# The first input of a trunk kernel arrives in blocks among the first weights, and its norm is applied to products instead of to the input

## The chip, the cores and the metric

The kernel runs on one NeuronCore of a Trainium2 chip. The core has a matrix engine (TensorE, PE in the rows; PEld is its loading of stationary operands), a vector engine (VectorE, DVE), a scalar engine (ScalarE, ACT), GpSimd (POOL) and SyncE (SP), which here only issues DMAs. The metric is the device time of one execution, in microseconds (us); lower is better.

## The reference, cut to what matters

Two layers over 256 tokens of width 2048, all in fp32. Layer 0 mixes tokens by a gated DeltaNet, layer 1 by sparse attention, and each mixer is followed by a squared-ReLU MLP. The change touches the first lines of layer 0:

```python
u = x * rsqrt(mean(x * x, -1) + EPS) * norm_mix[0]
proj = u @ w_in                       # 2048 -> 12352
qkv, z, b, a = split(proj, ...)       # qkv: 16 + 16 + 32 heads of 128; z: 4096; b, a: 32 each
qkv = silu(causal_conv(qkv, conv_w))
beta = sigmoid(b)
g = -exp(a_log) * softplus(a + dt_bias)
o = chunk_gated_delta_rule(l2norm(q), l2norm(k), v, g, beta)
o = rms_norm(o, out_norm) * silu(z)
x = x + o @ w_out
```

The factor `rsqrt(mean(x * x) + EPS)` is one number per token, so it can be applied to the rows of `x`, or to the products `x @ w_in` of that token.

## The kernel before

Every fp32 matrix is cut into a high and a low part (`split`: ACT rounds to `xhi` or `whi`, DVE subtracts and leaves `xlo` or `wlo`), and each product is three matmuls, high by high, high by low and low by high (`mm3`).

**Weights.** `Stream` holds a list of items, one per 512 KB of weights in the order of use. SP's queue loads an item into one of four `raw` buffers; an item of a gate group is three DMAs (128, 128 and 256 columns). ACT and DVE split it into one of four pairs `whi` and `wlo`. `get` hands out an item and emits loads up to seven items ahead and splits up to three ahead.

**Where DMAs wait.** The build gives each DMA issued by SP or ACT one of eight semaphores in turn (DMAHW0 to DMAHW7 below), and a DMA that comes to a semaphore again waits until the DMA that had it before has landed.

**Start.** SP first loads `x` into `xin` (four DMAs of 128 x 1024), the identity `ident` and the small vectors, and then the first weights. ACT and DVE form the sums of squares, DVE the norm `rs`. `normalise` scales `xin` in place, 512 columns at a time. `first` is a generator: for each of 16 slices k of 128 columns, PE transposes both token blocks into an `aux` bank of PSUM (there are two, in turn), and ACT and DVE split the bank into `xhi` and `xlo`. It calls `normalise` for the next 512 columns on the way. Below, T*k* is the pair of transposes of slice k, A*k* the 12 matmuls of the first group on slice k (4 channel tiles x 3), and item *i* the i-th item of weights; items 0 to 7 are the first group's. `by_channel` with `ahead=3` puts T(k+3) ahead of Ak in PE's order.

**Groups.** 16 groups of two value heads follow. Each computes q, k and v by `by_channel` (8 items, 192 matmuls into two `acc` banks), copies them to `s` (ACT), computes its gate z by `by_token` (4 items, 96 matmuls), and adds the generator `delta` for the group to `Background`, which emits its steps among the next groups' matmuls, at times that a small model of the engines (`Pace`) decides at build time. In group 0, two items between q, k, v and z give the decay inputs (48 matmuls), and the generator `decays` turns them into `tokc`, for which PE transposes the tile `E`; `delta` of group 0 waits for it. There are four `acc` banks. The engines run what the build emitted, each in its own order.

Counted over the PE order, the first group's q, k and v are matmuls 1 to 192 into `acc`, the decay inputs 193 to 240, z of group 0 241 to 336, and group 1's q, k and v 337 to 528.

Of the kernel before, what the change touches and what calls it, by code (L numbers as in the profile page):

```python
# [127 lines left out]
class Stream:  # L128
# [11 lines left out]

    def get(self):
# [3 lines left out]
        while self.split < min(i + ahead + 1, len(self.items)) or self.loaded < min(i + self.loads + 1, len(self.items)):  # L145
            while self.loaded < min(self.split + self.loads - self.ahead, len(self.items)):
                (n, w), pieces, _ = self.items[self.loaded]
                raw = self.raw_pool.tile([P, 1024], F32, name="raw")
                view = raw[:, : n * w].rearrange("p (n w) -> p n w", n=n)
                for at, src in pieces:  # L150
                    self.sync.dma_start(out=at(view), in_=src)
                self.raw[self.loaded] = raw
                self.loaded += 1
# [20 lines left out]
def tile_hybrid_trunk(ctx: ExitStack, tc: tile.TileContext, a: dict, out: bass.AP):  # L174
# [219 lines left out]

    with tc.tile_pool(name="first", bufs=1) as fp:
        xin = fp.tile([P, 2, D], F32, name="xin")
        rows = fp.tile([P, P], F32, name="rows")
# [43 lines left out]

        normalise(0)

        def first():
# [612 lines left out]
```

## Time and profile before

| | |
|---|---|
| median of 3 runs | 2621.61 us (2621.15 to 2622.31) |
| the profiled execution's own time | 2621.18 us |
| its span in the profile | 2619.4 us |
| PE busy | 2583.4 us, 99% of the span |
| DVE busy | 1539.8 us, 59% |
| ACT busy | 1288.2 us, 49% |
| POOL busy | 332.9 us, 13% |

The own time is 1.8 us above the span. PE is busy nearly throughout, so what matters is when it starts, where it stands still, and what it executes.

### The profile page before, as it was taken

To read this page: it belongs to the slowest core of one execution; us is meant where nothing else is said; L and a number is where in the kernel's file an instruction comes from. 1 tells how busy PE (TensorE), PEld (TensorE's weight loads), DVE (VectorE), ACT (ScalarE), POOL (GpSimd) and SP (SyncE) were. 2 spreads that over 40 slices of the span, in tenths; PEclk is the share of its full clock that TensorE was granted. 3 is DMA by queue.
4 is the path that set the end of the run, shared out by engine and by line. 5 is a ranking of instruction groups with operands and counts; after the bars stand their busy time and mean duration, and the time that the engine had idled before them with its cause. 6 is when DMAs were issued, how large, how long until landed. Compare 5 with 4: busy or idle time off the path is not lost.

```text
span 2619.4 us, 52870 instructions
## 1 busy us (share of the span) xinstructions
PE 2583.4 (99%) x21795; PEld 2356.7 (90%) x21795; DVE 1539.8 (59%) x2308; ACT 1288.2 (49%) x1992; POOL 332.9 (13%) x674
## 2 busy tenths in 40 slices
PE   7999999999999999999999999999999999999997
PEld 7999999999987899988899988898899988999886
DVE  5777677676764555554455545576555544555544
ACT  5555555555554444443344444566544433444443
POOL 0344434343441000000000000000000000000000
PEclk9999999999999999999999999999999999999999
DMA  6655455555544566666656666644566666666664
GB/s 191 187 142 146 132 150 143 154 142 142 148 165 154 183 184 195 194 199 193 194 177 188 195 192 187 185 129 147 176 192 193 194 193 193 191 187 186 193 193 137
DMA packets 325394, 455.95 MB, mean 174 GB/s; under 512 B 18280, under 2 KB 159840, under 8 KB 324768
## 3 DMA queue, kind: packets, MB, share of 16 engines
q1 hardware_dynamic: 321888, 443.85, 56.8%
q10 hardware_dynamic: 2928, 7.37, 0.8%
q8 instruction: 171, 2.80, 0.4%
q0 software_dynamic: 336, 1.34, 0.1%
q14 instruction: 71, 0.58, 0.1%
HBM read 450.37 MB, written 2.13 MB: 173 GB/s over the span
## 4 chain that ended last, share of the span: by engine, by line
PE 66%; DVE 1%; ACT 0%; issue 0%; ACTq 0%; DVEq 0%
PE acc L78 64%; PE aux L78 1%; PE pk L78 1%; DVE wlo L78 0%; DVE p L78 0%; DVE score L78 0%; ACT whi L78 0%; ACT h L78 0%; ACT acc L78 0%; DVE m L78 0%; DVE nm L78 0%; DVE h L78 0%; ACT p L78 0%; DVE rs_t L78 0%; DVE rs_u L78 0%
## 5 line engine op out<-in xcount | busy, mean ns | idle before, releaser
L78 DVE TENSOR_TENSOR wlo<-raw,whi 128x1024 fp32r<-128x1024 f32 x838 | 1024.4, 1229 | 870.6 <-ACT whi L78 862.7
L78 ACT CAST whi<-raw 128x1024 fp32r<-128x1024 f32 x838 | 873.9, 1049 | 844.1 <-PE acc L78 813.6
L78 PE MATMUL acc<-whi,h 128*128 128x512 f32 x2816 | 887.6, 392 | 2.1 <-ACT acc L78 2.1
L78 PE MATMUL acc<-xhi,whi 128*128 128x256 f32 x3088 | 876.1, 284 | 0.3 <-ACT whi L78 0.3
L78 PE MATMUL acc<-xhi,wlo 128*128 128x256 f32 x3088 | 860.7, 279 | 0.5 <-DVE wlo L78 0.5
L78 PE MATMUL acc<-xlo,whi 128*128 128x256 f32 x3088 | 861.1, 279 | 0.0
L78 PEld LDWEIGHTS acc<-whi,h 128*128 128x128 f32 x2816 | 528.8, 188 | 111.8 <-ACT acc L78 2.9
L78 PEld LDWEIGHTS acc<-xhi,wlo 128*128 128x128 f32 x3088 | 585.2, 190 | 0.8 <-DVE wlo L78 0.8
L78 PEld LDWEIGHTS acc<-xhi,whi 128*128 128x128 f32 x3088 | 581.3, 188 | 4.6 <-ACT whi L78 0.7
L78 PEld LDWEIGHTS acc<-xlo,whi 128*128 128x128 f32 x3088 | 582.2, 189 | 0.2
L78 PE MATMUL acc<-wlo,h 128*128 128x512 f32 x1408 | 548.3, 389 | 0.0
L78 PEld LDWEIGHTS acc<-wlo,h 128*128 128x128 f32 x1408 | 264.6, 188 | 52.7
L78 PE MATMUL acc<-whi,xhi 128*128 128x256 f32 (+2 forms) x576 | 173.7, 302 | 0.0
L78 PE MATMUL acc<-whi,xlo 128*128 128x256 f32 (+2 forms) x576 | 166.5, 289 | 0.0
L78 PE MATMUL acc<-wlo,xhi 128*128 128x256 f32 (+2 forms) x576 | 166.2, 289 | 0.0
L78 POOL DMA_DIRECT2D gain<-in_norm_final x1 | 0.6, 639 | 979.1 <-ACT p L78 979.1
L78 POOL TENSOR_SCALAR E<-R,tokc 128x128 f32<-128x128 f32 x96 | 88.1, 931 | 249.0 <-DMA R<-gl_dram 226.8
L78 DVE SCALAR_TENSOR_TENSOR y<-s,cw,y 128x255 f32<-128x255 f32 (+2 forms) x192 | 93.5, 488 | 41.4 <-ACT y L78 36.8
L78 PEld LDWEIGHTS acc<-whi,xhi 128*128 128x128 f32 x576 | 108.0, 187 | 3.6
L78 PEld LDWEIGHTS acc<-wlo,xhi 128*128 128x128 f32 x576 | 108.3, 188 | 1.3
L78 PEld LDWEIGHTS acc<-whi,xlo 128*128 128x128 f32 x576 | 108.1, 188 | 1.2
L78 POOL TENSOR_TENSOR h<-h,gain 128x512 f32<-128x512 f32 x8 | 10.1, 1284 | 776.9 <-ACT acc L78 776.9
(245 smaller groups left out, 1944.3 us busy)
## 6 DMA issues: line engine op xcount, KB each, us to landing
raw<-in_mlp_w_up SPq DMA_DIRECT2D x256, 512.0 KB, 4.4
raw<-in_mlp_w_down SPq DMA_DIRECT2D x256, 512.0 KB, 4.3
raw<-in_dn_w_in SPq DMA_DIRECT2D x66, 512.0 KB, 4.2
raw<-in_dn_w_in SPq DMA_DIRECT2D x256, 128.0 KB, 2.8
raw<-in_dn_w_in SPq DMA_DIRECT2D x128, 256.0 KB, 3.2
raw<-in_dn_w_out SPq DMA_DIRECT2D x64, 512.0 KB, 3.8
raw<-in_dsa_w_out SPq DMA_DIRECT2D x32, 512.0 KB, 4.1
raw<-in_dsa_w_uq SPq DMA_DIRECT2D x16, 512.0 KB, 3.7
```

Source lines behind the costliest of these rows:

```text
L78: r = f(*args, **kwargs)
```

## The change

`x` stays as it is. It is loaded as four blocks of 512 columns for all 256 tokens, each as one more DMA ahead of the weights of items 0, 1, 3 and 5. `ident` and the first 16 vector rows go to ACT's queue, the other seven vector loads come after item 3 on SP's. `first` transposes raw slices as soon as their block has been issued, and forms the norm afterwards: four `squares` steps, the sum, `rsqrt`, a diagonal `dg`, and a matmul of `ones` with `dg` that lays the norm along the columns of `rs_row`. `s` is then a product with `rs_row` (DVE, from PSUM) instead of a copy (ACT), in all 16 groups; z takes half the norm as the scale of its tanh; one more POOL product per group puts the norm into `f`; `decays` gets two more products. Group 0's decay and z matmuls now come before `bg.drain()`. Two runs of matmuls of `ones` with itself (12 and 8, `warm_up`) whose results are not used are added to PE.

```diff
+    def fetch(self):
+        while self.loaded < min(self.split + self.loads - self.ahead, len(self.items)):
+            (n, w), pieces, _ = self.items[self.loaded]
+            raw = self.raw_pool.tile([P, 1024], F32, name="raw")
+            view = raw[:, : n * w].rearrange("p (n w) -> p n w", n=n)
+            for at, src in pieces:
+                self.sync.dma_start(out=at(view), in_=src)
+            self.raw[self.loaded] = raw
+            self.loaded += 1
+
...
-            ws.add((2, 512), [
+            blocks = [slice(c * 512, c * 512 + 512) for c in range(4) if g == 0 and k // 2 == max(0, 2 * c - 1)]
+            ws.add((2, 512), [((lambda v, c=c: xin[:, :, c]), x_rows[:, :, c]) for c in blocks] + [
...
-        quarters = [(tb, slice(c * 1024, c * 1024 + 1024)) for c in range(2) for tb in range(2)]
-        for tb, s in quarters:
-            sync.dma_start(out=xin[:, tb, s], in_=a["x"][0, tb * P:tb * P + P, s])
-        sync.dma_start(out=ident, in_=a["consts"][:, 0:P])
-        dve.memset(rows, 0.0)
+        def warm_up(n):
+            warm = aux()
+            for _ in range(n):
+                pe.matmul(warm[:, 0:P], lhsT=ones, rhs=ones, start=True, stop=True)
+
+        warm_up(12)
+        act.dma_start(out=rows[0], in_=a["norm_mix"][0].rearrange("(n p) -> n p", p=P))
+        act.dma_start(out=ident, in_=a["consts"][:, 0:P])
+        pool.dma_start(out=cwr, in_=a["dn_conv_w"][0].rearrange("t (c p) -> (t c) p", p=P).rearrange("(n q) p -> q n p", q=P))
+        pool.dma_start(out=upper, in_=a["consts"][:, P:2 * P])
+        pool.dma_start(out=fine, in_=a["consts"][:, 2 * P:].rearrange("p (n c) -> p n c", c=B))
+
...
+        sq8 = small_tile(8, "sq8")
+        ws.fetch()
...
-            sync.dma_start(out=rows[at:at + n, :], in_=src.rearrange("(n p) -> n p", p=P))
+            if at:
+                sync.dma_start(out=rows[1][at - 16:at - 16 + n, :], in_=src.rearrange("(n p) -> n p", p=P))
...
-        sq4 = small_tile(4, "sq4")
-        for n, (tb, s) in enumerate(quarters):
-            junk = fp.tile([P, 1024], F32, name="junk", bufs=2)
-            if n % 2 == 0:
-                act.activation(junk, xin[:, tb, s], AF.Square, accum_out=sq4[:, n:n + 1])
-            else:
-                dve.scalar_tensor_tensor(junk, xin[:, tb, s], 1.0, xin[:, tb, s], op0=OP.mult, op1=OP.mult, accum_out=sq4[:, n:n + 1])
-        rs = small_tile(2, "rs")
-        sq = small_tile(2, "sq")
-        dve.tensor_tensor(sq, sq4[:, 0:2], sq4[:, 2:4], op=OP.add)
-        dve.tensor_scalar(sq, sq, 1.0 / D, EPS, op0=OP.mult, op1=OP.add)
-        rsqrt(rs, sq, 2)
-        tp = aux()
-        pe.transpose(tp[:, 0:P], rows, ident)
-        act.copy(vecs, tp[:, 0:72])
-
...
+        def vectors(i, s):
+            tp = aux()
+            n = s.stop - s.start
+            pe.transpose(tp[:, 0:n], rows[i], ident[0:n, 0:n])
+            act.copy(vecs[:, s], tp[:, 0:n])
+
+        vectors(0, slice(0, 16))
+
+        def squares(c):
             s = slice(c * 512, c * 512 + 512)
-            act.activation(xin[:, 0, s], xin[:, 0, s], AF.Copy, scale=rs[:, 0:1])
-            dve.tensor_scalar(xin[:, 1, s], xin[:, 1, s], rs[:, 1:2], None, op0=OP.mult)
-
-        normalise(0)
+            junk = fp.tile([P, 2, 512], F32, name="junk", bufs=2)
+            act.activation(junk[:, 0], xin[:, 0, s], AF.Square, accum_out=sq8[:, c:c + 1])
+            dve.scalar_tensor_tensor(junk[:, 1], xin[:, 1, s], 1.0, xin[:, 1, s], op0=OP.mult, op1=OP.mult,
+                                     accum_out=sq8[:, 4 + c:5 + c])
...
             for k in range(KD):
+                while ws.loaded <= max(0, k // 4 * 2 - 1):
+                    yield
...
                 ready.add(("x0", k))
-                if k % 4 == 1 and k < 12:
-                    normalise(k // 4 + 1)
-                yield
+                yield
+            for c in range(4):
+                squares(c)
+                yield
+            sq = small_tile(2, "sq")
+            dve.tensor_reduce(sq, sq8.rearrange("p (b c) -> p b c", b=2), axis=AX.X, op=OP.add)
+            dve.tensor_scalar(sq, sq, 1.0 / D, EPS, op0=OP.mult, op1=OP.add)
+            rsqrt(rs0, sq, 2)
+            dg = fp.tile([P, 2, P], F32, name="dg")
+            for tb in range(2):
+                dve.tensor_scalar(dg[:, tb], ident, rs0[:, tb:tb + 1], None, op0=OP.mult)
+            yield
+            t = aux()
+            pe.matmul(t[:, :T], lhsT=ones, rhs=dg.rearrange("p b c -> p (b c)"), start=True, stop=True)
+            act.copy(rs_row, t[:, :T])
+            yield
...
+            vectors(1, slice(16, 72))
...
         bg.step()
+        warm_up(8)
         first_banks = by_channel(8, x_part, "x0", ahead=3)
+        first_ba = by_channel(2, x_part, "x0", n_ct=1)[0]
+        first_zo = by_token(4, x_part, "x0", n_cols=256)
         bg.drain()
...
+        dve.tensor_scalar(rs_half, rs0, 0.5, None, op0=OP.mult)
...
-            act.activation(ba[64:96], ps[64:96, :T], AF.Tanh, scale=0.5)
+            dve.tensor_tensor(ba[64:96], ps[64:96, :T], rs_row[64:96], op=OP.mult)
+            act.activation(ba[64:96], ba[64:96], AF.Tanh, scale=0.5)
...
-            dve.tensor_scalar(xa, ps[q, :T], par[q, 1:2], None, op0=OP.add)
+            dve.tensor_tensor(xa, ps[q, :T], rs_row[q], op=OP.mult)
+            dve.tensor_scalar(xa, xa, par[q, 1:2], None, op0=OP.add)
...
             pool.tensor_tensor(pair(f), pair(f), rep(sc), op=OP.mult)
+            pool.tensor_tensor(pair(f), pair(f), rep(rs0), op=OP.mult)
...
-                act.copy(s[:, 2 * c:2 * c + 2].rearrange("p n t -> p (n t)"), banks[c])
+                dve.tensor_tensor(s[:, 2 * c:2 * c + 2], banks[c].rearrange("p (n t) -> p n t", n=2),
+                                  rs_row.unsqueeze(1).to_broadcast([P, 2, T]), op=OP.mult)
             if g == 0:
-                bg.add(decays(by_channel(2, x_part, "x0", n_ct=1)[0]))
-            zo = by_token(4, x_part, "x0", n_cols=256)
...
-                act.activation(zg[:, b], zo[b], AF.Tanh, scale=0.5)
+                act.activation(zg[:, b], zo[b], AF.Tanh, scale=rs_half[:, b:b + 1])
```

On SP's queue, ahead of the first weights before the change, and between item 3 (`raw_141`) and item 5 (`raw_189`) after it. Before:

```order
L411 DMA rows_98<-in_norm_mlp 16x128 [waits DMAHW0_49]
L411 DMA rows_98<-in_dsa_q_norm 4x128 [waits DMAHW1_49]
L411 DMA rows_98<-in_dsa_kv_norm 2x128 [waits DMAHW2_49]
L411 DMA rows_98<-in_dsa_kidx_norm 1x128 [waits DMAHW3_49]
L411 DMA rows_98<-in_dn_out_norm 1x128 [waits DMAHW4_49]
L151 DMA raw_162<-in_dn_w_in 128x2x128 [waits DMAHW5_49]
L151 DMA raw_162<-in_dn_w_in 128x2x128 [waits DMAHW6_49]
L151 DMA raw_162<-in_dn_w_in 128x2x256 [waits DMAHW7_49]
```

After:

```order
L147 DMA raw_141<-in_dn_w_in 128x2x256 [waits DMAHW0_49]
L436 DMA rows56_106<-in_norm_mlp 16x128 [waits DMAHW1_49]
L436 DMA rows56_106<-in_norm_mix 16x128 [waits DMAHW2_49]
L436 DMA rows56_106<-in_norm_mlp 16x128 [waits DMAHW3_49]
L436 DMA rows56_106<-in_dsa_q_norm 4x128 [waits DMAHW4_49]
L436 DMA rows56_106<-in_dsa_kv_norm 2x128 [waits DMAHW5_49]
L436 DMA rows56_106<-in_dsa_kidx_norm 1x128 [waits DMAHW6_49]
L436 DMA rows56_106<-in_dn_out_norm 1x128 [waits DMAHW7_49]
L147 DMA raw_181<-in_dn_w_in 128x2x128 [waits DMAHW0_49,DVE_49]
L147 DMA raw_181<-in_dn_w_in 128x2x128 [waits DMAHW1_49]
L147 DMA raw_181<-in_dn_w_in 128x2x256 [waits DMAHW2_49]
L147 DMA xin_104<-in_x 128x2x512 [waits DMAHW3_49]
```

Before, all of `x` and the small vectors stood ahead of the first weights. Now the small vectors stand behind item 3, and the first load of item 4 (`raw_181`) waits for the semaphore of item 3's last load.

On DVE's queue, the two weight splits of items 4 and 5 and what stands behind them, before and after. Before (`raw_182` and `raw_190` are items 4 and 5; `aux_297` and `aux_314` hold T7 and T8):

```order
L78 TENSOR_TENSOR wlo_286<-raw_182,whi_285 128x1024 [waits DMAHW2_49,DMAHW3_49,DMAHW1_49,Activation_49]
L78 TENSOR_TENSOR wlo_292<-raw_190,whi_291 128x1024 [waits DMAHW5_49,DMAHW4_49,DMAHW6_49,PE_49,Activation_49]
L78 SCALAR_TENSOR_TENSOR xlo_93<-aux_297,vecs_85,xhi_92 128x256 [waits Activation_49]
L78 SCALAR_TENSOR_TENSOR xlo_93<-aux_314,vecs_85,xhi_92 128x256 [waits Activation_49]
L78 TENSOR_TENSOR wlo_332<-raw_237,whi_331 128x1024 [waits DMAHW1_49,DMAHW0_49,DMAHW7_49,PE_49,Activation_49]
L78 SCALAR_TENSOR_TENSOR xlo_93<-aux_337,vecs_85,xhi_92 128x256 [waits Activation_49]
```

After (`raw_181` and `raw_189` are items 4 and 5; `aux_295` and `aux_312` hold T7 and T8):

```order
L78 TENSOR_TENSOR wlo_284<-raw_181,whi_283 128x1024 [waits DMAHW1_49,DMAHW2_49,DMAHW0_49,Activation_49]
L78 TENSOR_TENSOR wlo_290<-raw_189,whi_289 128x1024 [waits DMAHW5_49,DMAHW4_49,DMAHW6_49,PE_49,Activation_49]
L78 SCALAR_TENSOR_TENSOR xlo_93<-aux_295,vecs_85,xhi_92 128x256 [waits Activation_49]
L78 SCALAR_TENSOR_TENSOR xlo_93<-aux_312,vecs_85,xhi_92 128x256 [waits Activation_49]
L78 TENSOR_TENSOR wlo_330<-raw_237,whi_329 128x1024 [waits DMAHW1_49,DMAHW0_49,DMAHW7_49,PE_49,Activation_49]
```

The order of splits is the same in both: item 5's split stands ahead of slice 7's. Only the in-place scaling (`xin`) is gone. T9 uses the `aux` bank that T7 had, and so waits for slice 7's split.

On DVE's queue at the end of group 0 after the change (`raw_565` is item 16; `acc_175` and `acc_176` are the two banks of the first group; before, ACT copied them as soon as the 192 matmuls were done):

```order
L78 TENSOR_TENSOR wlo_614<-raw_453,whi_613 128x1024 [waits DMAHW2_49,PE_49,Activation_49]
L78 TENSOR_TENSOR wlo_646<-raw_491,whi_645 128x1024 [waits DMAHW4_49,DMAHW5_49,DMAHW3_49,Activation_49]
L78 TENSOR_TENSOR wlo_688<-raw_527,whi_687 128x1024 [waits DMAHW6_49,DMAHW0_49,DMAHW7_49,PE_49,Activation_49]
L78 TENSOR_TENSOR wlo_720<-raw_565,whi_719 128x1024 [waits DMAHW2_49,DMAHW3_49,DMAHW1_49,Activation_49]
L78 TENSOR_SCALAR rs_half_99<-rs0_98 128x2
L78 TENSOR_TENSOR s_757<-acc_175,rs_row_100 128x512
L78 TENSOR_TENSOR s_757<-acc_176,rs_row_100 128x512
L78 SCALAR_TENSOR_TENSOR zg_760<-zg_760,acc_612 128x256 [waits Activation_49] x2
```

The products that free the two banks now stand behind item 16's split, and group 1's first matmuls take these two banks. On PE, the transposes of `E` stand behind `acc` matmul 444 before (inside group 1's q, k and v) and behind 576 after (inside its z); the matmul with `dg` stands behind 276, and the transposes of `cwr` and of the other vectors behind 288 (`cwr`: 168 before). The first products of `delta` for groups 0 to 4 stand 144, 132, 108, 72 and 42 `acc` matmuls later than before; from group 5 on they stand where they stood.

## Rows read from the trace of the kernel before

**Rows 1.** PE's waits over the whole span: total us, times, longest.
```profile
PE aux L78 <- DVE rs_t L78: 13.0, 1, 13.0
...
PE aux L78 <- DVE E L78: 1.5, 1, 1.5
```

**Rows 2.** Timeline of the start: start us, length us, engine, what, idle before and releaser.
```profile
0.73 1.81 SPq L401 DMA_DIRECT2D xin<-in_x  x4
...
5.34 0.31 SPq L411 DMA_DIRECT2D rows<-in_norm_mlp  x1
5.34 1.06 ACT L78 ACTIVATE junk<-xin 128x1024 f32<-128x1024 f32 x1 [3.33 <-DMA xin<-in_x]
...
10.79 0.22 SPq L411 DMA_DIRECT2D rows<-in_dsa_kidx_norm  x1
...
11.36 45.74 SPq L151 DMA_DIRECT2D raw<-in_dn_w_in  x42
...
20.04 0.58 PE L78 MATMUL acc<-xhi,wlo 128*128 128x256 f32 x1 [0.47 <-DVE wlo L78]
```

**Rows 3.** Windows of the start: last column GB/s moved, before it DMA share.
```profile
0.00:5.00 5.00, 0.00 (x0) 0.00 (x0) 0.31 (x2) 1.28 (x1) 3.23 (x9) 1.00 0.54 160
...
15.00:20.00 5.00, 3.03 (x10) 1.83 (x10) 2.78 (x6) 4.16 (x8) 0.00 (x0) 1.00 0.97 275
...
5.00:9.00 4.00, 0.00 (x0) 0.00 (x0) 1.23 (x2) 1.15 (x2) 0.00 (x0) 1.00 1.01 371
...
12.30:15.00 2.70, 0.44 (x1) 0.18 (x1) 2.25 (x14) 0.43 (x2) 0.00 (x0) 1.00 0.88 229
...
17.00:20.00 3.00, 1.91 (x6) 1.11 (x6) 2.36 (x5) 3.00 (x6) 0.00 (x0) 1.00 1.08 325
```

**Rows 4.** Timeline of PE: neighbours at 25 us, and fp32 products at 243 us.
```profile
24.69 0.41 PE L78 MATMUL acc<-xhi,whi 128*128 128x256 f32 x1
...
24.90 0.36 PE L78 MATMUL acc<-xlo,whi 128*128 128x256 f32 x1
...
25.69 0.28 PE L78 MATMUL acc<-xhi,wlo 128*128 128x256 f32 x1
...
243.80 0.71 PE L78 MATMUL aux<-r,Tt 128*128 128x128 f32 x4
...
244.27 0.36 PE L78 MATMUL acc<-xhi,whi 128*128 128x256 f32 x1
```

**Rows 5.** Timeline of PE: T8 and T9, and `acc` matmuls 192 and 193.
```profile
30.11 0.38 PE L78 MATMUL aux<-wide,xin 128*128 128x128 f32 x2
...
31.74 0.38 PE L78 MATMUL aux<-wide,xin 128*128 128x128 f32 x2
...
47.52 0.28 PE L78 MATMUL acc<-xhi,wlo 128*128 128x256 f32 x1
47.63 0.28 PE L78 MATMUL acc<-xhi,whi 128*128 128x256 f32 x1
```

**Rows 6.** Timeline of PE: `acc` matmul 444, and the transposes of `E`.
```profile
76.73 0.28 PE L78 MATMUL acc<-xhi,wlo 128*128 128x256 f32 x1
78.53 0.44 PE L78 MATMUL aux<-wide,E 128*128 128x128 f32 x2 [1.52 <-DVE E L78]
```

**Rows 7.** Groups by form up to 700 us (`h<-acc`: 700 to 1640): busy us, mean ns of one, idle before and releasers.
```profile
L78 DVE TENSOR_TENSOR wlo<-raw,whi 128x1024 fp32r<-128x1024 f32 x186 | 229.4, 1238 | 112.7 <-ACT whi L78 106.0 <-DMA raw<-in_dn_w_in 5.1 <-DMA R<-gl_dram 0.9
...
L78 DVE SCALAR_TENSOR_TENSOR xlo<-aux,vecs,xhi 128x256 fp32r<-128x256 f32 x16 | 7.2, 479 | 3.4 <-ACT xhi L78 3.4
...
L78 ACT CAST whi<-raw 128x1024 fp32r<-128x1024 f32 x186 | 193.2, 1047 | 62.9 <-PE acc L78 50.8 <-DVE E L78 4.8 <-ACT y L78 4.0
...
L78 DVE TENSOR_TENSOR h<-acc,h 128x512 f32<-128x512 f32 x8 | 5.0, 682 | 0.0
...
L78 POOL TENSOR_TENSOR f<-f,sc 128x4 f32<-128x4 f32 x12 | 2.4, 201 | 0.9
```

**Rows 8.** One window of the groups: busy us of PE, PEld, DVE, ACT, POOL.
```profile
310.00:410.00 100.00, 100.00 (x1371) 94.14 (x1365) 68.55 (x155) 57.37 (x122) 42.59 (x93) 1.00 0.52 144
```

More of the change, by code (lines that the diff above doesn't have):

```diff
@@ L145, in get @@
         while self.split < min(i + ahead + 1, len(self.items)) or self.loaded < min(i + self.loads + 1, len(self.items)):
[L146 to L153, printed above, removed]
+            self.fetch()
             if self.split >= min(i + ahead + 1, len(self.items)):
@@ L213, in tile_hybrid_trunk @@
     QO, KO, VO, ZO, BO = 0, 2048, 4096, 8192, 12288
+    x_rows = a["x"][0].rearrange("(b p) d -> p b d", p=P)
     for g in range(DN_G):
         for k in range(0, KD, 2):
-            ws.add((2, 512), [
+            blocks = [slice(c * 512, c * 512 + 512) for c in range(4) if g == 0 and k // 2 == max(0, 2 * c - 1)]
+            ws.add((2, 512), [((lambda v, c=c: xin[:, :, c]), x_rows[:, :, c]) for c in blocks] + [
                 (lambda v: v[:, :, 0:128], w_in[:, k:k + 2, KO + g * 128:KO + g * 128 + 128]),
@@ L392, in two_chunks, with vec @@
         return [by_token(2, h_part(tiles), key, outs=o, k0=nk - 4) for o in outs]
+    carry = ExitStack()
+    carried = carry.enter_context(tc.tile_pool(name="carried", bufs=1))
+    tokc = carried.tile([P, 2, P], F32, name="tokc")
+    rs0 = carried.tile([P, 2], F32, name="rs0")
+    rs_half = carried.tile([P, 2], F32, name="rs_half")
+    rs_row = carried.tile([P, T], F32, name="rs_row")
     with tc.tile_pool(name="first", bufs=1) as fp:
         xin = fp.tile([P, 2, D], F32, name="xin")
-        rows = fp.tile([P, P], F32, name="rows")
+        rows = [fp.tile([n, P], F32, name=f"rows{n}") for n in (16, 56)]
         cwr = fp.tile([P, 2, P], F32, name="cwr")
-        quarters = [(tb, slice(c * 1024, c * 1024 + 1024)) for c in range(2) for tb in range(2)]
-        for tb, s in quarters:
-            sync.dma_start(out=xin[:, tb, s], in_=a["x"][0, tb * P:tb * P + P, s])
-        sync.dma_start(out=ident, in_=a["consts"][:, 0:P])
-        dve.memset(rows, 0.0)
+        def warm_up(n):
[8 more added lines that the diff above has]
+        pool.dma_start(out=fine, in_=a["consts"][:, 2 * P:].rearrange("p (n c) -> p n c", c=B))
+        def vec(name, i=0):
+            return vecs[:, VEC[name] + i:VEC[name] + i + 1]
+        sq8 = small_tile(8, "sq8")
+        ws.fetch()
         at = 0
@@ L410, in tile_hybrid_trunk @@
             n = src.shape[0] // P
-            sync.dma_start(out=rows[at:at + n, :], in_=src.rearrange("(n p) -> n p", p=P))
+            if at:
+                sync.dma_start(out=rows[1][at - 16:at - 16 + n, :], in_=src.rearrange("(n p) -> n p", p=P))
             VEC[name] = at
             at += n
-        pool.dma_start(out=cwr, in_=a["dn_conv_w"][0].rearrange("t (c p) -> (t c) p", p=P).rearrange("(n q) p -> q n p", q=P))
-        pool.dma_start(out=upper, in_=a["consts"][:, P:2 * P])
-        pool.dma_start(out=fine, in_=a["consts"][:, 2 * P:].rearrange("p (n c) -> p n c", c=B))
@@ L418, in vec @@
-        def vec(name, i=0):
-            return vecs[:, VEC[name] + i:VEC[name] + i + 1]
-        sq4 = small_tile(4, "sq4")
-        for n, (tb, s) in enumerate(quarters):
-            junk = fp.tile([P, 1024], F32, name="junk", bufs=2)
-            if n % 2 == 0:
-                act.activation(junk, xin[:, tb, s], AF.Square, accum_out=sq4[:, n:n + 1])
-            else:
-                dve.scalar_tensor_tensor(junk, xin[:, tb, s], 1.0, xin[:, tb, s], op0=OP.mult, op1=OP.mult, accum_out=sq4[:, n:n + 1])
@@ L428, in tile_hybrid_trunk @@
-        rs = small_tile(2, "rs")
-        sq = small_tile(2, "sq")
-        dve.tensor_tensor(sq, sq4[:, 0:2], sq4[:, 2:4], op=OP.add)
-        dve.tensor_scalar(sq, sq, 1.0 / D, EPS, op0=OP.mult, op1=OP.add)
-        rsqrt(rs, sq, 2)
-        tp = aux()
-        pe.transpose(tp[:, 0:P], rows, ident)
-        act.copy(vecs, tp[:, 0:72])
-        def normalise(c):
+        def vectors(i, s):
[3 more added lines that the diff above has]
+            act.copy(vecs[:, s], tp[:, 0:n])
@@ L461, in tile_hybrid_trunk @@
         bg.step()
+        warm_up(8)
         first_banks = by_channel(8, x_part, "x0", ahead=3)
+        first_ba = by_channel(2, x_part, "x0", n_ct=1)[0]
+        first_zo = by_token(4, x_part, "x0", n_cols=256)
         bg.drain()
-    tokc = const.tile([P, 2, P], F32, name="tokc")
     GLM, BETA, GL = 32, 64, 96
@@ L719, in tile_hybrid_trunk @@
             for c in range(2):
-                act.copy(s[:, 2 * c:2 * c + 2].rearrange("p n t -> p (n t)"), banks[c])
+                dve.tensor_tensor(s[:, 2 * c:2 * c + 2], banks[c].rearrange("p (n t) -> p n t", n=2),
+                                  rs_row.unsqueeze(1).to_broadcast([P, 2, T]), op=OP.mult)
             if g == 0:
-                bg.add(decays(by_channel(2, x_part, "x0", n_ct=1)[0]))
-            zo = by_token(4, x_part, "x0", n_cols=256)
+                bg.add(decays(first_ba))
+            zo = by_token(4, x_part, "x0", n_cols=256) if g else first_zo
             if g > 2:
@@ L738, in tile_hybrid_trunk @@
     spare[:] = [None, "pk0", None, "pk1"]
+    carry.close()
     res = ctx.enter_context(tc.tile_pool(name="res", bufs=1, reuse_waits="tile"))
```

## The prediction

> **What bounds the kernel now.** I read the waits of PE first. PE is busy for 99% of the span, as the table has it; 13.0 us of waiting lie ahead of its first instruction, and 1.5 us at the tile `E`, in group 1 [rows 1]. In the groups PE is busy for 100 of 100 us while DVE has 31 us to spare [rows 8]. So this change can gain what PE loses at the start, and it loses wherever it stops PE anew.
>
> The timeline of the start shows why PE is late. SP loads `x` from 0.73 us on, then the small vectors, and issues the first weights only at 11.36 us [rows 2]. The eight semaphores do that: SP's next vector load is issued at 5.34 us, in the moment in which ACT's wait for the first piece of `x` ends, so a DMA that takes a semaphore over waits for the landing of the one before. PE's stream without gaps begins at 20.04 us [rows 2], and it begins at half rate: neighbours start 0.21 us apart up to 24.90 us, against 0.11 us later [rows 4, 5]. These are the 1.2 and the 2.4 GHz level; the column of the granted clock says 1.00 throughout [rows 3] and doesn't show it. T9 then starts at 31.74 us, and the first matmul behind group 0's q, k and v at 47.63 us [rows 5].
>
> **Where T9 goes.** I place the new start by T9, because what follows it is known: from T9 to 47.63 us are 15.89 us without a wait [rows 5]. In that stretch stands the pair of `cwr`, which moves away. From 47.63 to 76.73 us PE starts 251 matmuls, 0.116 us each [rows 5, 6]; a slice takes 31.74 - 30.11 = 1.63 us, so a pair of transposes costs 1.63 - 12 x 0.116 = 0.24 us. Without it, T9 to the end of q, k, v is 15.65 us.
>
> T9 waits for the split of slice 7, which stands on DVE behind the split of item 5, so it waits for item 5 to land. How late is that?
>
> Bytes: a block of `x` and an item are 524 KB each; `cwr`, `upper`, `fine`, `ident` and 16 vector rows are 370 KB by their shapes. Up to 5 us the queues moved 160 GB/s, that is 800 KB; later 371 GB/s (`x` in long rows) and 325 GB/s (weights in short rows, queue full) [rows 3]. Blocks now have rows of 2 KB, between the two kinds; I take 325.
>
> - Item 3's last load comes after 3 blocks and 4 items: 3670 + 370 - 800 = 3240 KB, 10.0 us at 325 GB/s, so at 15.0 us. The same count for the fourth piece of `x` before gives 9.5 us (800 KB, then 371 GB/s); it landed at 10.79 us, when SP's waiting load went out [rows 2]. Last pieces trail by up to 1.3 us; I take 0.7, hence 15.7 us.
> - Only then does SP issue item 4, since seven small loads hold the other semaphores. The queue is empty, and it starts as it did before at 11.36 us: nothing for a while, then 229 GB/s from 12.3 to 15.0 us, 620 KB in 3.6 us [rows 2, 3]. Items 4, 5 and the last block are 1570 KB: 620 by 19.3 us, 950 more at 325 GB/s, so item 5 lands at 22.2 us.
> - Behind it: its cast 1.05, its subtraction 1.24, slice 7's `xlo` 0.48 us [rows 7], and some 0.2 us of hand-offs, my estimate. T9 at 25.2 us.
>
> PE is there earlier. T4 waits in the same way for item 1 (2 blocks, 2 items: 1670 KB after 5 us, 10.1 us, with the trailing about 10.6) and starts some 3.0 us later, at 13.6; five slices on, PE is ready for T9 at 13.6 + 5 x 1.63 = 21.8 us and waits 3.4 us. What the first `warm_up` costs lies ahead of that. An fp32 product of 128 columns costs 0.235 us at the fast level (two in 0.47 us, four records) [rows 4], about 0.43 at the slow one: 12 of them run from about 1 to 6.2 us, 0.9 us past the landing of block 0 (as the first piece before, 5.3 us). The 8 others cost 1.9 to 3.5 us. At worst A0 ends at 14.5 us instead of before 13.6; the wait at T9 swallows it. Without that wait it would cost the 0.9 us. So the warm-ups are worth their faster clock only up to T9.
>
> Then q, k, v end at 25.2 + 15.65 = 40.85 us, **6.8 us earlier** than 47.63. The bounds: at 371 GB/s T9 comes at 23.6 us and the gain is 8.4; at 275 GB/s, the mean of 15 to 20 us in which that queue also ran dry [rows 3], T9 comes at 27.6 and the gain is 4.4.
>
> **What follows, to the transposes of `E`.** Added on PE: the product with `dg`, 256 columns, 0.47 us [rows 4]; the pair of `cwr`, 0.24, and of the vectors, half of that, 0.12. The norm itself runs beside group 0's decay and z products; its chain of two-column operations may take until matmul 276, 84 matmuls or 9.7 us behind the end of q, k, v, which I take as cover enough. New wait: group 1's first matmul needs the bank that the first product `s` frees, and this stands behind the split of item 16, which needs the buffer of item 12. PE leaves item 12 with 24 matmuls to go, 2.8 us; cast 1.05, subtraction 1.24, product 0.68 (the nearest row, DVE from PSUM) [rows 7] and 0.3 us of hand-offs are 3.3. It waits 0.5 us, bounds 0 and 1.5. The wait at `E`, 1.52 us [rows 6], moves from matmul 444 to 576. Queued on DVE ahead of `E` are now group 1's two products (1.4 us), one subtraction (1.24) and seven small operations; PE runs 48 matmuls, 5.6 us, meanwhile. I take 0.2 us of wait, bounds 0 and the old 1.5. Sum: 0.47 + 0.24 + 0.12 + 0.5 + 0.2 - 1.52 = 0.0 us, bounds -0.7 and +2.3.
>
> **The other 15 groups.** DVE gets two products of 0.68 us a group, 22 us in all, ACT loses its copies, POOL gets 0.2 us a group [rows 7]. A group lasts at least 33 us (288 matmuls by 0.116), and DVE's 31 idle us in 100 [rows 8] cover 1.4 us of it, and the banks are not wanted again before the group's 96 z matmuls, 11 us, are through. So I cost it at nothing; if the cover were gone it would be the whole 22 us. `decays` and the first `delta` come 132 matmuls later in PE's order, and the later groups have caught up with the old order by group 5. From there on PE executes what it did.
>
> **Sum.** 2621.2 (the profiled execution's own time) - 6.8 + 0.0 = **2614.4 us**; the median of the three runs is 0.4 us above that execution, which I don't add.
>
> **Rivals.**
> - *Transfers keep ahead* (chance 0.12): if items 4 and 5 land by 18.8 us, PE alone decides; T9 at 21.8, q, k, v end at 37.45, 10.2 us gained, 2611.0. For it: before, no load is among PE's long waits. Against it: SP's queue empties behind item 3, as it did between `x` and the weights.
> - *Transfers are slow* (0.14): 275 GB/s or worse, 2616.8 to 2618.
> - *The clock falls again* (0.07): PE stands for 3.4 us at T9. The longest stand in the groups, 1.5 us, left PE at the fast spacing afterwards; a longer one is not in the trace. If it falls, PE runs slow from T9 as it did from 20.04 to 24.90 us [rows 2, 4] and loses half of 4.9 us, 2.4: 2616.8. The Trainium skill, TensorE: Matmul & The Clock Gate, section "HAM oscillation — how this bites in real kernels", says that waits for DMA between short bursts of matmuls throttle the clock again, each time at its price; by that rule this rival holds, and the dummy products at the start would be paid for twice. No run here shows a stand of that length.
> - *DVE becomes late* (0.04): `s` now queues behind subtractions. If each group exposed its 1.4 us to PE, 22 us would come and the time be 2636, slower. It takes 0.43 us a group to eat the gain. Against it: PE waits for DVE hardly at all in the groups, at 69% busy.
>
> **Numbers.** Chance of my forecast 0.63, its own range 2612.5 to 2616. The range to hold 8 in 10 reaches to the first rival and to slow transfers: 2610.8 to 2617.6. A change of 0.2%, 5.2 us, is about what a measurement of this kernel tells from none. Faster by more, below 2616.0: the forecast's 0.63 nearly whole, the first rival, 0.74 together. Within 0.2%: slow transfers, the clock and a rest of the forecast, 0.22. Slower: 0.04.
>
> **What would show it.** First weights issued near 1.2 us; item 4 issued near 15.7 us, with a hole in the transfers behind it; PE waiting at T9 (`aux<-wide,xin`) for DVE `xlo` for 2 to 5 us; neighbours 0.21 us apart only in the first microseconds; q, k, v ending near 41 us; a wait of about 0.5 us for the bank of `s`, and none to speak of at `E`. If PE waits elsewhere in the groups, or T9 doesn't wait, the step is wrong.

## The result and the profile after

The changed kernel takes 2636.7 us (median of 4 runs, 2635.7 to 2637.8) beside 2621.8 us for the kernel before (4 runs): ratio 1.0059, 95% interval 1.0046 to 1.0072. It is slower by 15 us, where 2614.4 was forecast. The profiled span grew by 15.6 us, from 2619.4 to 2635.0.

PE's waits over the span of the changed kernel, in the columns of [rows 1]:

```profile
PE aux L78 <- DVE xlo L78: 6.9, 3, 4.0
PE acc L78 <- ACT acc L78: 2.1, 2, 1.0
PE aux L78 <- DVE r L78: 1.8, 3, 1.0
PE aux L78 <- DVE Tc L78: 1.2, 2, 0.8
PE aux L78 <- DVE ones L78: 1.1, 1, 1.1
PE aux L78 <- DMA wide<-in_consts: 0.7, 1, 0.7
PE aux L78 <- DVE E L78: 0.5, 1, 0.5
...
PE acc L78 <- DVE s L78: 0.4, 1, 0.4
```

The 13.0 us for `rs_t` are gone, and no wait of that size has taken their place. Over the whole span PE stands idle for 29.9 us, against 36.0 before, so the loss is not a wait. PE's busy time says where to look: 2583.4 us before, 2605.1 us now.

The timeline of the start, to be held against [rows 2, 4, 5, 6]: SP's issue of item 4 and what follows it, T4, T9, the casts of items 4 and 5 on ACT, the end of q, k, v, and the transposes of `E`:

```profile
15.77 0.40 SPq L147 DMA_DIRECT2D raw<-in_dn_w_in  x1
...
18.30 0.47 SPq L147 DMA_DIRECT2D xin<-in_x  x1
18.87 0.41 SPq L147 DMA_DIRECT2D raw<-in_dn_w_in  x1
...
20.83 1.05 ACT L78 CAST whi<-raw 128x1024 fp32r<-128x1024 f32 x1 [1.05 <-DMA raw<-in_dn_w_in]
25.17 1.04 ACT L78 CAST whi<-raw 128x1024 fp32r<-128x1024 f32 x1 [3.28 <-DMA raw<-in_dn_w_in]
...
14.01 0.44 PE L78 MATMUL aux<-wide,xin 128*128 128x128 f32 x2 [2.07 <-DVE xlo L78]
...
14.74 0.42 PE L78 MATMUL acc<-xhi,whi 128*128 128x256 f32 x1
14.95 0.41 PE L78 MATMUL acc<-xlo,whi 128*128 128x256 f32 x1
...
27.92 0.50 PE L78 MATMUL aux<-wide,xin 128*128 128x128 f32 x2 [3.97 <-DVE xlo L78]
...
28.65 0.41 PE L78 MATMUL acc<-xhi,wlo 128*128 128x256 f32 x1
28.86 0.41 PE L78 MATMUL acc<-xhi,whi 128*128 128x256 f32 x1
...
45.22 0.28 PE L78 MATMUL acc<-xhi,whi 128*128 128x256 f32 x1
...
92.29 0.41 PE L78 MATMUL aux<-wide,E 128*128 128x128 f32 x2 [0.50 <-DVE E L78]
```

Behind both waits, T4's and T9's, the neighbours are 0.21 us apart, the 1.2 GHz level: the clock fell twice. The column of the granted clock shows it too, with 0.71 from 15 to 20 us and 0.84 from 30 to 35 us. q, k and v of group 0 end at 45.22 us, 2.4 us earlier than before, not 6.8.

To place the other 18 us, I take two waits for ACT that stand in both kernels at the same matmul, ahead of the two MLPs. First the kernel before, then the changed one:

```profile
859.59 0.50 PE L78 MATMUL acc<-whi,h 128*128 128x512 f32 x1 [1.04 <-ACT acc L78]
...
1854.15 0.50 PE L78 MATMUL acc<-whi,h 128*128 128x512 f32 x1 [1.04 <-ACT acc L78]
```

```profile
861.29 0.50 PE L78 MATMUL acc<-whi,h 128*128 128x512 f32 x1 [1.04 <-ACT acc L78]
...
1863.10 0.50 PE L78 MATMUL acc<-whi,h 128*128 128x512 f32 x1 [1.04 <-ACT acc L78]
```

| stretch | before, us | after, us | difference |
|---|---|---|---|
| to the end of q, k, v of group 0 | 47.63 | 45.22 | -2.4 |
| on to the first of these waits | 811.96 | 816.07 | +4.1 |
| on to the second, with the first MLP | 994.56 | 1001.81 | +7.3 |
| on to the end, with the second MLP | 765.25 | 771.90 | +6.7 |

Fourteen of the 15.6 us are lost in code that the change doesn't touch and whose order on PE is the same. Windows inside the first and the second half of the first MLP's up-projection (columns as in [rows 8]) show how. First the kernel before, then the changed one:

```profile
980.00:1080.00 100.00, 100.00 (x885) 100.00 (x884) 54.84 (x54) 47.56 (x53) 0.00 (x0) 1.00 0.64 200
1340.00:1440.00 100.00, 100.00 (x852) 100.00 (x851) 55.32 (x55) 47.39 (x55) 0.00 (x0) 1.00 0.60 184
```

```profile
980.00:1080.00 100.00, 100.00 (x852) 100.00 (x851) 55.01 (x53) 46.04 (x53) 0.00 (x0) 1.00 0.62 190
1340.00:1440.00 100.00, 100.00 (x851) 100.00 (x851) 54.09 (x52) 45.24 (x51) 0.00 (x0) 1.00 0.62 189
```

PE is 100% busy in all four at clock 1.00, with nothing but `by_channel`'s matmuls: weights `whi` or `wlo` stationary, 256 columns of `xhi` or `xlo` moving. Yet one window holds 885 of them and three hold 852. Taken from the distances of neighbouring starts, the pace is 113.3 ns a matmul in the first half before, and 117.8 ns in the second half and in both halves after. A half has 1536 such matmuls, and 1536 x 4.45 ns = 6.8 us, in each of two MLPs. That is the loss. It was not among the rivals.

### The profile page after: what moved, and what is told of

Its sections match the earlier page's. It is cut to its first block, busy times and chain, and to the rows that moved or that the text cites. A ratio compares the mean times of both kernels' runs of the same rounds, so it can differ in the third digit from the quotient of the medians.

```text
span 2635.0 us, 53002 instructions
## 1 busy us (share of the span) xinstructions
PE 2605.1 (99%) x21838; PEld 2377.1 (90%) x21838; DVE 1568.7 (60%) x2344; ACT 1275.2 (48%) x1962; POOL 335.7 (13%) x690
## 4 chain that ended last, share of the span: by engine, by line
PE 66%; DVE 1%; ACT 0%; issue 0%; ACTq 0%; DVEq 0%
PE acc L78 64%; PE aux L78 1%; PE pk L78 1%; DVE wlo L78 0%; DVE p L78 0%; DVE score L78 0%; ACT whi L78 0%; ACT h L78 0%; ACT acc L78 0%; DVE m L78 0%; DVE nm L78 0%; DVE h L78 0%; ACT p L78 0%; DVE rs_t L78 0%; DVE rs_u L78 0%
```

## Experiments

A time without a number of runs is that of one execution. "Beside" gives the kernel before on the same chip (2620.0 to 2622.1 us).

**What sets the pace?** Between the two builds two things differ in the MLPs: the PSUM banks of `acc` (pairs 0,1 and 2,3 before; 0,2 and 1,3 after) and the SBUF addresses. `tokc` left one of the pools in front and `sq8` entered another, so `raw`, `whi`, `wlo` and `h` lie 896 bytes lower (the first `whi` at 39072 instead of 39968), while `xhi` stays. These addresses are the build's; the profile holds none. (The expectation of e2_addr names other numbers, 51360 and 52256; they too are 896 apart and lie 160 and 32 beyond a multiple of 256.)

e1_banks (on the changed kernel; e4_before_banks has the same line in the kernel before):

```diff
+        dve.memset(acc()[:, 0:1], 0.0)
         first_ba = by_channel(2, x_part, "x0", n_ct=1)[0]
```

> The changed kernel with one small write (DVE, one column) into a bank of acc ahead of group 0's decay matmuls, so that the banks are handed out from group 1 on as in the kernel before; nothing else moves. Theory PACE: the 15 us are lost in matmuls of 256 columns that run at 117.8 ns apiece where the kernel before ran half of them at 113.3 ns, and what decides between the two paces is the pair of PSUM banks; then both first halves of the MLPs (1536 matmuls each) return to 113.3 ns and the time falls by some 14 us to about 2622. If the banks don't decide, the time stays at 2636 +- 2. Theory DVE LATE (the products s in the groups make PE wait): 2636 +- 2 too, and PE's pace doesn't change.

Measured 2635.4 beside 2620.1; 117.8 ns in all four halves. The banks don't decide.

> The kernel before with the same small write into a bank of acc ahead of group 0's decay matmuls: from group 1 on its banks are those of the changed kernel (pairs 0,2 and 1,3 in the MLPs instead of 0,1 and 2,3). PACE by banks: the MLPs' first halves fall to 117.8 ns, +14 us, about 2636. PACE by addresses or by what ran before, and DVE LATE: 2622 +- 1.

Measured 2620.4 beside 2620.1; 113.3 and 117.8 ns as before. The same answer from the other side.

e2_addr:

```diff
+    tokc = const.tile([P, 2, P], F32, name="tokc")
...
-    tokc = carried.tile([P, 2, P], F32, name="tokc")
...
-        sq8 = small_tile(8, "sq8")
+        sq8 = fp.tile([P, 8], F32, name="sq8")
```

> The changed kernel with tokc and sq8 kept in other pools, so that raw, whi, wlo and h lie at the SBUF addresses of the kernel before (52256 instead of 51360 for the first whi); order and banks are untouched. Theory PACE by addresses: the MLPs' first halves return to 113.3 ns a matmul, about 2622. PACE by banks or by what ran before: 2636 +- 2. DVE LATE: 2636 +- 2.

Measured 2622.7 beside 2620.1. The windows of e2_addr are those of the kernel before:

```profile
980.00:1080.00 100.00, 100.00 (x885) 100.00 (x884) 56.07 (x54) 47.11 (x53) 0.00 (x0) 1.00 0.64 200
1340.00:1440.00 100.00, 100.00 (x852) 100.00 (x851) 54.43 (x54) 47.02 (x55) 0.00 (x0) 1.00 0.61 185
```

Two tiles in other pools, and 14 us are back, with all that the change does still in place. They come from the MLPs, where the last two stretches of the table take 994.7 and 765.2 us again; from the end of q, k, v to the first MLP it still takes 815.6 us.

e3_copy leaves the norm out of q, k and v:

```diff
-                dve.tensor_tensor(s[:, 2 * c:2 * c + 2], banks[c].rearrange("p (n t) -> p n t", n=2),
-                                  rs_row.unsqueeze(1).to_broadcast([P, 2, T]), op=OP.mult)
+                act.copy(s[:, 2 * c:2 * c + 2].rearrange("p n t -> p (n t)"), banks[c])
```

> The changed kernel with s copied by ACT as before instead of multiplied by rs_row on DVE (the norm is left out of q, k and v). Theory DVE LATE: the groups give their 15 us or more back, 2621 or less, and the gain lies between 60 and 850 us of the span. Theory PACE: the groups give back at most 2 us and the time is 2634 to 2636, unless the pace of the MLPs' matmuls happens to return to 113.3 ns, which the trace would show at 960 us.

Measured 2638.8, beside 2620.1. Nothing came back: DVE's products aren't the loss, and the MLPs' stretches take what they take in the changed kernel (1001.9 and 771.9 us). Waits for `r` (1.8 us) and `Tc` (0.9) are there without the products.

**Which address?** A pad ahead of `raw` shifts `raw`, `whi`, `wlo` and `h` of the changed kernel; *n* is 8 floats in e5_pad32 and e6_pad32_32, 32 in e7_pad128, 128 in e8_pad512, 48 in e9_pad192, 40 in e10_pad160, 24 in e11_pad96 and f1_dist. e6_pad32_32 and f1_dist also lower `xhi` and `xlo` by 32 bytes.

```diff
+    pad = const.tile([P, n], F32, name="pad")
+    dve.memset(pad[:, 0:1], 0.0)
...
+    edge = ctx.enter_context(tc.tile_pool(name="edge", bufs=1, side="right")).tile([P, 8], F32, name="edge")
+    dve.memset(edge, 0.0)
```

> The changed kernel with one tile of 32 bytes a partition added ahead of raw, whi, wlo and h, so that these begin on multiples of 64 bytes (whi at 39104; before 39968, changed 39072, both 32 beyond a multiple of 64). Order and banks are untouched, xhi and xlo stay. ADDRESS theory: the pace of by_channel's matmuls depends on where the stationary parts lie. If the place within 64 bytes matters, the matmuls take another pace than 113.3 and 117.8 ns, or the quicker of the two throughout (both halves of both MLPs, 2607); if only the class that the kernel before had matters, it stays at 117.8 ns and 2636. HISTORY theory (what PE ran before decides, addresses don't): 2636.

> As e5_pad32, and xhi and xlo moved by 32 bytes too, so that the moving operands also begin on multiples of 64 bytes. If the moving operand's place costs something (a 256-column matmul takes 272 clock periods of 2.4 GHz at 113.3 ns, 16 more than its columns), the pace falls below 113.3 ns, at most to 106.7 ns, and the time below 2600. If not, as e5_pad32.

> The changed kernel with 128 bytes added: whi at 39200, which agrees with the kernel before within 256 bytes (both 32 beyond a multiple) but not within 512. If the class within 256 bytes decides, the MLPs' first halves run at 113.3 ns and the time is 2622 +- 2; if it takes the exact address or a longer period, 2636.

> The changed kernel with 512 bytes added: whi at 39584, which agrees with the changed kernel within 512 bytes (160 beyond a multiple of 256) but lies elsewhere. If the class within 256 or 512 bytes decides, 117.8 ns throughout and 2636 +- 2; if a shift of any kind resets the pace, some other time between 2607 and 2636.

> The changed kernel with 192 bytes added ahead of raw, whi, wlo and h: xhi lies 128 beyond whi, counted within 256 bytes (192 in the kernel before and in e7_pad128, 64 in the changed kernel and e8_pad512, 32 in e5_pad32, 0 in e6_pad32_32). CONFLICT theory: the weight load and the moving operand are read at the same time, and the pace depends on the distance between their addresses within 256 bytes; 0 was the slowest (120.0 ns), so the distance farthest from 0 should be the quickest: 113.3 ns in both halves of both MLPs, 2608 +- 3. CLASS theory (only the place of whi counts): some pace between 113.3 and 120.0 ns, no reason for 2608.

> As e9_pad192 with 160 bytes: distance 160. CONFLICT theory: 113.3 ns at least as often as at 192, so 2608 to 2623. CLASS theory: 113.3 to 120.0 ns without an order; whi on a multiple of 64 gave 116.7 ns at e5_pad32 (2636).

> As e9_pad192 with 96 bytes: distance 224, that is 32 on the other side of 0. CONFLICT theory, if it counts the distance alike on both sides: as e5_pad32, 116.7 ns and 2636. If it counts the order of the two: another pace, up to 120.0 ns.

> The changed kernel with 96 bytes added ahead of whi and 32 bytes taken from the far side for xhi, so that whi lies where it did in e11_pad96 (39168, a multiple of 256; 118.3 ns, 2647.4) and xhi 192 beyond it within 256 bytes, as in the kernel before and e7_pad128. If the distance between the two decides: 113.3 and 117.8 ns in the MLPs' halves and 2623 +- 2. If the place of whi alone decides: 118.3 ns and 2647 +- 2. If both places count by themselves: something else.

Measured, with the distance from `whi` to `xhi` counted within 256 bytes, and the pace in windows inside the first and second halves (alike in both MLPs):

| kernel | `whi` in 256 | distance | ns, first half | ns, second half | us |
|---|---|---|---|---|---|
| before | 32 | 192 | 113.3 | 117.8 | 2620.0 to 2622.1 |
| e2_addr | 32 | 192 | 113.3 | 117.8 | 2622.7 |
| e7_pad128 | 32 | 192 | 113.3 | 117.8 | 2622.8 |
| f1_dist | 0 | 192 | 117.8 | 117.8 | 2633.1 |
| changed | 160 | 64 | 117.8 | 117.8 | 2636.7 |
| e8_pad512 | 160 | 64 | 117.8 | 117.8 | 2635.8 |
| e5_pad32 | 192 | 32 | 116.7 | 116.7 | 2635.8 |
| e11_pad96 | 0 | 224 | 118.3 | 118.3 | 2647.4 |
| e10_pad160 | 64 | 160 | 117.3 | 118.7 | 2649.8 |
| e9_pad192 | 96 | 128 | 118.7 | 120.0 | 2655.7 |
| e6_pad32_32 | 192 | 0 | 120.0 | 120.0 | 2663.2 |

The slowest has this window:

```profile
980.00:1080.00 100.00, 100.00 (x836) 100.00 (x835) 52.66 (x52) 45.21 (x51) 0.00 (x0) 1.00 0.60 182
```

The place within 256 bytes counts: `whi` of e7_pad128 agrees with that of the kernel before within 256 bytes but not within 512, `whi` of e8_pad512 with that of the changed kernel within 512, and each runs at that kernel's paces in the MLPs. For the changed kernel 40 us lie between the best and the worst place. That a multiple of 64 would help proved wrong (e5_pad32, e6_pad32_32), and so did "the farther apart the quicker": 128 was nearly the slowest.

f1_dist missed both forecasts, 2623 us by the distance and 2647 by the place of `whi`. Its trace says more than its time. In the first half of each MLP four pairs of transposes stand among the first 84 matmuls; the first 12 matmuls run at 117.8 ns, and behind the four pairs the pace is 113.5, 117.8, 113.8 and 117.8 ns, in both MLPs alike. So both paces of distance 192 occur, each pair switches between them, and the last one leaves the slow pace for the 1,452 matmuls to come. In its groups (50 to 720 us) neighbours in `by_channel` are 114.6 ns apart on the mean, like e2_addr's 115.1, while e11_pad96, with `whi` in the same place, has 118.3. So the place of `whi` alone doesn't decide. The distance fits the paces that occur, in this one check of it, but doesn't say which of two holds.

f4_before_pad128 is the kernel before with *n* = 32 and nothing else:

> The kernel before with 128 bytes added ahead of raw, whi, wlo and h, nothing else: the distance within 256 bytes becomes 64, as in the changed kernel. If the addresses make the 15 us by themselves, both halves of both MLPs run at 117.8 ns and the time is 2620.1 + 2 x 7 = 2634, up to 2637 with the groups. If the changed order is needed too: 2620.

Measured 2633.9 beside 2622.1, 117.8 ns in all halves:

```profile
980.00:1080.00 100.00, 100.00 (x851) 100.00 (x850) 53.33 (x52) 45.76 (x52) 0.00 (x0) 1.00 0.63 192
1340.00:1440.00 100.00, 100.00 (x852) 100.00 (x851) 53.95 (x52) 45.65 (x52) 0.00 (x0) 1.00 0.61 188
```

The address alone makes the kernel before 11.8 us slower, without any part of the change.

**Two paces at one address.** At distance 192 both 113.3 and 117.8 ns occur. Each half enters behind 512-column matmuls at 117.8 ns. In the first halves the four pairs of transposes (of `h`) stand between the first matmuls. In the kernel before the pace is 113.3 ns from the first pair on, and it stays so for the 1,452 matmuls behind the last pair, 164 us. f2_nudge (on e12_vec_pool, below) adds two pairs of transposes of `ident` to the second halves, g1_nudge_h (on f3_no_warm, below) four pairs of the first half's own transposes of `h`, as shown here:

```diff
+    def nudge():
+        for i in range(4):
+            t = aux()
+            for tb in range(2):
+                pe.transpose(t[:, tb * P:tb * P + P], h[:, tb, (12 + i) * P:(13 + i) * P], ident)
+            yield
...
+            if half == 1:
+                bg.add(nudge())
             for p in range(8):
```

> As e12_vec_pool (2616.2), and in the second half of each MLP two pairs of transposes whose results are not used stand behind the first 12 and 24 matmuls, as the transposes of xT do in the first half. HYSTERESIS theory: at this distance both paces hold once entered; the stretch enters at 117.8 ns behind the 512-column matmuls and the transposes knock it to 113.3 ns, as the first halves show at 951 to 961 us of the kernel before. Then 2 x 1512 matmuls run 4.4 ns quicker, less 0.6 us for the transposes: 2616.2 - 13.4 + 1 = 2604 +- 2. If the second halves are slow for another reason (their place in the program, what DVE and ACT do beside them): 2616 to 2618.

Measured 2618.9 beside 2622.1. Two pairs ran in each second half, and it stayed at 117.8 ns behind both; 2604 us, the time if they had worked, was not reached.

> As f3_no_warm (2617.0 beside 2622.1 for the kernel before), and in the second half of each MLP four pairs of transposes of h (the columns that the first half transposes last), whose results are not used, behind the first 12, 24, 36 and 48 matmuls. HYSTERESIS theory with the first half's own transposes: the second halves run at 113.3 ns from there on, 2 x 1488 x 4.4 ns = 13.2 us less, 1 us more for the transposes: 12 us below g2_best. If something else makes the first halves quick: 1 us above g2_best.

Measured 2604.4 (5 runs), ratio to the kernel before 0.9935, interval 0.9922 to 0.9947, and 11.1 us below g2_best. Its windows:

```profile
980.00:1080.00 100.00, 100.00 (x884) 100.00 (x884) 55.87 (x56) 48.14 (x56) 0.00 (x0) 1.00 0.64 195
1340.00:1440.00 100.00, 100.00 (x884) 100.00 (x884) 57.03 (x56) 49.24 (x56) 0.00 (x0) 1.00 0.62 194
```

Eight transposes whose results nobody reads turn 117.8 into 113.3 ns for the 1,488 matmuls behind them, in each MLP. The first of the four pairs already does it: the 12 matmuls ahead of it run at 117.8 ns, the 12 behind it at 113.8. f2_nudge's two pairs of `ident` stood at the first two of these places and changed nothing, so the number of pairs isn't what makes the difference. What is left between them is the tile that they read.

**The start.** e12_vec_pool is e7_pad128 with the vector loads on another queue; f3_no_warm is e12_vec_pool without the lines `warm_up(12)` and `warm_up(8)`; g2_best is f3_no_warm again, timed.

```diff
-                sync.dma_start(out=rows[1][at - 16:at - 16 + n, :], in_=src.rearrange("(n p) -> n p", p=P))
+                pool.dma_start(out=rows[1][at - 16:at - 16 + n, :], in_=src.rearrange("(n p) -> n p", p=P))
```

> As e7_pad128 (2622.8, the quick place for whi), and the seven small vector loads go to POOL's queue instead of SP's, where they stood between the loads of items 3 and 4. Theory HOLE: these loads made SP issue item 4 only at 15.8 us, the transfers fell to 107 GB/s between 15 and 20 us, and T9 waited 4.0 us for item 5's split (27.9 us), whereupon PE ran 3.4 us at half rate. Without them item 4 is issued near 11 us, T9 starts near 23.8 us with a wait below 1 us, the second stretch at 0.21 us spacing goes, and the time falls by 4 to 6 us to 2617 to 2619. Rival, the QUEUE is full anyway (bytes decide): T9 moves by less than 1.5 us, and the time by less than 2.

Measured 2616.2 beside 2620.1, and 6.7 us below e7_pad128. Its windows of the transfers, the last line of each fence from 15 to 20 us, first the changed kernel, then e12_vec_pool, and T9 and the end of q, k, v of the latter:

```profile
10.00:15.00 5.00, 2.93 (x24) 2.65 (x23) 2.42 (x5) 2.30 (x5) 0.00 (x0) 0.95 1.06 319
15.00:20.00 5.00, 5.00 (x33) 5.00 (x33) 3.42 (x5) 2.79 (x4) 0.00 (x0) 0.71 0.41 107
```

```profile
10.00:15.00 5.00, 3.19 (x28) 2.92 (x27) 2.28 (x5) 2.54 (x5) 0.00 (x0) 1.00 1.12 332
15.00:20.00 5.00, 5.00 (x46) 5.00 (x45) 4.46 (x6) 3.51 (x5) 0.00 (x0) 1.00 1.11 335
```

```profile
24.68 0.44 PE L78 MATMUL aux<-wide,xin 128*128 128x128 f32 x2 [2.65 <-DVE xlo L78]
...
40.12 0.28 PE L78 MATMUL acc<-xhi,whi 128*128 128x256 f32 x1
```

The hole is filled, T9 comes 3.2 us earlier than in the changed kernel, and q, k, v end 5.1 us earlier. In e7_pad128, which differs in the seven loads alone, T9 starts at 28.11 us and q, k, v end at 46.21, 6.1 us later than in e12_vec_pool; T9 makes 3.4 of these; behind T9, e7_pad128 ran two stretches at 0.21 us spacing and e12_vec_pool none. The wait at T9 shrank but stayed, at 2.65 us, where less than 1 was expected.

> As e12_vec_pool (2616.2) without the two runs of dummy products. The prediction costed them as worth their faster clock only up to T9. If the clock rises only while PE works, T0 to the first products run at half rate, some 2 to 4 us behind, but A0 need not wait for 8 dummy products: T4 still waits for item 1 (13.8 us), and T9 for items 4 and 5 (24.7 us). So if the waits decide, 2616 +- 1.5; if the clock decides, 2618 to 2620.

Measured 2617.0 beside 2622.1. The first products run 0.21 us apart, T9 stands at 24.53 us without a wait, and q, k, v end at 39.84 us; with the dummy products they ended at 40.12 (e12_vec_pool) and 41.76 (f2_nudge, the same program up to there). So the dummy products buy nothing here: PE's slower start only uses up the wait at T9.

> The changed kernel with 128 bytes added ahead of whi, the seven vector loads on POOL's queue and no dummy products, as f3_no_warm: 2617 beside 2622 for the kernel before, ratio 0.998 with an interval of about 0.001 to either side; faster by 0.2% if the single look was right, or 0.1 to 0.3%.

Measured 2615.5 (11 runs), ratio 0.9977, interval 0.9968 to 0.9986: faster than the kernel before by 0.2%.

## Why the prediction was wrong

The profiled execution took 2636.8 us, 22.4 more than forecast: 13.9 in the two MLPs, which had no term, 4.4 at the start, which gained 2.4 instead of 6.8, and 4.1 between the start and the first MLP, which was put at 0.0.

**The step that failed** is the last sentence on the 15 groups: "From there on PE executes what it did." It executes the same matmuls in the same order, but at another pace. The prediction read 0.116 us from [rows 5, 6] as the price of such a matmul. It was a mean over stretches at 113.3 and at 117.8 ns, and what moves it, where the tiles lie, is in the part of the diff that I took for bookkeeping (`tokc` leaves its pool). The missing term is 14 us; e2_addr gives it back, and f4_before_pad128 makes most of it without the change. Why the place of the tiles sets the pace stays open. The Trainium skill, SBUF — State Buffer, section "Who interferes with whom", says that PE reads moving operand and weights through two independent ports and that only the port pair shared by DVE and GpSimd causes contention. By that a pad costs nothing; the runs disagree, by 11.8 us for 128 bytes. That the two reads disturb each other is the reading that suggests itself, and no run shows it directly.

**The start.** Item 4 was issued at 15.77 us (15.7 forecast), T4 began at 14.01 (13.6), and the wait at T9 was 3.97 us (3.4). But T9 came at 27.92, not 25.2: I let items 4 and 5 and the last block follow at once, as weights did before at 11.36 us. They went out one by one: the block at 18.30 us, item 5 from 18.87 us on, and its cast began at 25.17, where 22.2 was forecast. The term that was mis-sized is the restart of the queue (columns as in [rows 3]):

```profile
15.77:19.37 3.60, 3.60 (x25) 3.60 (x24) 2.75 (x3) 1.61 (x4) 0.00 (x0) 0.70 0.39 92
```

In 3.6 us 92 GB/s bring 330 KB, where 620 were forecast. T9 comes about when the rival of slow transfers had it (27.6), but not for its reason: from 20 to 25 us the queues moved 302 GB/s. e12_vec_pool shows the cause: without the seven small loads on SP's queue T9 comes at 24.68.

**The clock** fell as well, the rival with 0.07. T9 to the end of q, k, v took 17.3 us where 15.65 were forecast, so 1.65 us against the 2.4 given there. Here the trace agrees with what the prediction quotes from the Trainium skill, TensorE: Matmul & The Clock Gate, section "HAM oscillation — how this bites in real kernels", that such waits throttle the clock again. It doesn't agree everywhere: e12_vec_pool waits 2.65 us at T9 and needs 15.44 us to the end of q, k, v, without a fall.

**The new waits.** The bank for `s` cost 0.4 us (0.5 forecast), `E` 0.5 (0.2). Not forecast: waits for `r` and `Tc`, most of them in the early groups, 3.0 us together, where the kernel before has 0.5 for the same tiles. (The 1.1 us for `ones` stand ahead of the first dummy product and cost nothing.) That `decays` and the first `delta` come 132 matmuls later was costed at nothing. These 2.5 us more, 0.4 for `s`, 1.0 less at `E` and the 0.83 of the added products make 2.7 of the 4.1 us lost up to the first MLP; the rest stays open. Most of the waits are in e3_copy too, without DVE's products, so I put them down to the order, which no run changed by itself. The addresses aren't the cause of this part: e2_addr keeps 3.7 of the 4.1 us.

**DVE late**, the rival on the other side, named 2636 us, and the measured time is that. Its mechanism is not what happened: DVE is busier, as forecast (74.6 of 100 us from 310 to 410 us, against [rows 8]), and PE waits 0.2 us for it there; e3_copy settles it. A rival whose time comes true isn't thereby shown.

## What to carry to other kernels

When a change moves a tile between pools, compare addresses too, and compare PE's count of matmuls in a window of pure matmul work far behind the change: at equal busy share and clock, 885 against 852 in 100 us stood for 14 of the 15.6 us. A price taken as a mean over a stretch should first be looked at for two values. Small loads on a queue of eight shared semaphores belong where no large load stands behind them.

## What the runs showed of the hardware

- A stream of 256-column matmuls in which every one brings new weights ran at 113.3 to 120.0 ns apiece, depending on where stationary and moving operand lie within 256 bytes. The streams with 512 moving columns took 226.7 ns in all of these kernels, twice 113.3.
- At distance 192 the pace has two values, and a stretch keeps the one it has entered for 164 us and 1,452 matmuls, until other work comes between. In the groups both 113 and 118 ns occur at distance 64 as well. Of the neighbouring starts in `by_channel` between 50 and 720 us, 34% are at most 115.5 ns apart in the changed kernel and 58% in the kernel before; in `by_token` it is the other way, 63% and 15%. Over both kinds the mean is 115.9 ns in either kernel, so the groups lose nothing by the pace. Why transposes of `h` change the pace and transposes of `ident` don't, and why each pair switches it in f1_dist while in the kernel before the first does and the others leave it, is open.
- The clock's fall isn't a property of the program alone: e12_vec_pool and f2_nudge have the same program up to the second half of the first MLP, and q, k, v ended at 40.12 us in the one and at 41.76 in the other, on another chip, which ran two stretches at 0.21 us spacing. Behind a wait of 2.0 to 2.1 us at T4 a stretch of that spacing came in the changed kernel, e8_pad512 and e9_pad192, and none in e3_copy and e10_pad160.
